# A two-layer encoder on one core: bank numbering in the down-projection, row norms in two steps, and transfers on another queue

## The chip, the cores and the metric

The kernel runs on one core of a Trainium2 chip as one program. The metric is the device time of one execution in microseconds; before the change the median of three runs is 3454.63 us (3453.96 to 3462.44).

## The reference

1024 tokens of width 1024 in float32, two layers. Each layer has four kinds of attention side by side (A dilated windows, B latent, C differential, D two-dimensional neighbourhoods), an output projection, a gated MLP of width 2816 with a convolution over three tokens, and a gated embedding. In short:

```python
for i in range(DEPTH):                                   # 2 layers
    hn = rms_norm(h, attn_norm[i])
    cols = hn @ w_in[i]                                  # 1024 -> A | B | C | D columns
    a_cols, b_cols, c_cols, d_cols = jnp.split(cols, split_at, axis=-1)
    o_a = dilated_mixture(rope(qa, pos), rope(ka, pos), va)
    o_b = mla_mixer(b_cols, mla_q_norm[i], w_uq[i], mla_kv_norm[i], w_ukv[i], pos)
    o_c = diff_mixer(c_cols, ..., diff_subln[i], lam_init, pos)   # (softmax1 - lam*softmax2) @ v, then rms_norm
    o_d = neighbourhood_attn(qd, kd, vd, na_rpb[i])      # windows of a 16 x 64 grid, with a bias table
    mix = jnp.concatenate([merge_heads(o) for o in (o_a, o_b, o_c, o_d)], axis=-1)
    h = h + mix @ w_o[i]
    hn = rms_norm(h, ffn_norm[i])
    u = dwconv_centred(hn @ w_up[i], conv_w[i], conv_b[i])        # 1024 -> 2 x 2816
    gate, val = jnp.split(u, 2, axis=-1)
    h = h + (jax.nn.gelu(gate) * val) @ w_down[i]        # 2816 -> 1024
    e = p[i] @ w_ple_proj[i]
    g = jax.nn.sigmoid(rms_norm(h, ple_norm[i]) @ w_ple_gate[i])
    h = h + g * e
return rms_norm(h, final_norm)
```

`rms_norm` divides a row by the root of its mean square and multiplies it by a gain.

## The kernel before

Tokens lie in NT = 8 tiles of 128 rows. A float32 product is made of three matmuls of rounded operands: each operand is split into a part `hi` and a remainder `lo` (`whi`, `wlo` of a weight by GpSimd, lines 111 and 112; `ah`, `al` of an activation by ScalarE and VectorE, lines 1242 and 1243; `xh`, `xl` of a transposed row, lines 162 and 163), and line 181 multiplies hi by hi, lo by hi and hi by lo. TensorE's results go to three kinds of banks, `psM`, `psT` (128 x 512, two of each) and `psS` (128 x 1024, two).

The MLP's down-projection takes the 2816 hidden columns as 11 chunks of two blocks of 128. For each chunk `down_tile` (line 1293) goes over the eight token tiles: twelve matmuls of 128 x 512 fill both halves of a bank, and VectorE adds them to `h` (line 1299). While one chunk is computed, `act_load` and `down_w` fetch and split the activations and weights of later ones. The last chunk (`down_last`) is joined with what follows: after its tile `t`, the row's norm is computed, its transpose follows, and then a quarter of the embedding's gate (`gate`, line 1321). At the end of a layer the last quarter of the gate is followed by the next layer's first norm, transpose and input projection, or, in the last layer, by the final norm and the store to `out`.

`norm_rows` (line 147) is a chain over three engines: ScalarE squares the row and sums it (line 149), GpSimd makes the reciprocal root (lines 137 and 139), VectorE scales the row (line 151); then TensorE transposes it (line 161). `norm_a` calls it, and `pipeline(n, *stages)` (line 999) writes out a list of functions as a software pipeline: in step `s`, stage `k` handles tile `s - k`.

The attention streams run beside the input projections. Differential attention (C) handles heads in two pairs; after the second head of a pair, GpSimd makes the pair's normalised output `c_ob` (line 450) and SP issues eight stores of it to the rows of `mix` in memory (line 453). Then the neighbourhood stream (D) loads two masks (lines 812 and 814), four bias tables `d_T` (line 825), to which VectorE adds a mask (line 826), and the tiles `d_x` (line 831), which TensorE transposes (line 835). GpSimd's queue already issues one kind of store, `mix<-b_ob` (line 569).

Pools, engines and dependencies are written by hand, but a framework schedules: it may place an instruction of an engine before others that were written earlier.

Of the kernel before, what the change touches and what calls it, by code (L numbers as in the profile page):

```python
# [19 lines left out]
P = 128  # L20
# [25 lines left out]
def kernel(ctx: ExitStack, tc: tile.TileContext, a, out, dbg=None):  # L46
# [19 lines left out]
    def small(n, name):  # L66
        return sm.tile([P, n], F32, name=name, tag=f"{name}_{n}")
# [77 lines left out]
        return g  # L145

    def norm_rows(ht, gB, hn):
        ss = small(1, "ss")
        se.activation(hn, ht, AF.Square, scale=1.0 / 32.0, accum_out=ss)  # L149
        r = rstd(ss, EPS, 1)  # L150
        ve.scalar_tensor_tensor(hn, ht, r[:, 0:1], gB, op0=ALU.mult, op1=ALU.mult)  # L151

    def transpose_split(src, hi, lo, nk, bank):

# [195 lines left out]
    def attn_C(c, L, cd, mix):  # L350
# [77 lines left out]
        def finish(h, g, st, turn):  # L428

            pair, hh = h // 2, h % 2  # L430
            if g == 0:
                st["ob"] = osp.tile([P, NT, 64], F32, name="oh", tag="oh")
            oh = st["ob"]
            turn(oh[:, 2 * g:2 * g + 2])
            if g < 3:
                return
            if hh == 0:
                obs[pair] = osp.tile([P, NT, 2, 64], F32, name="c_ob", tag="c_ob")
            ob = obs[pair]
            r1 = small(8, "r1")  # L440
            ve.reciprocal(r1, st["ss"])
            ge.tensor_tensor(oh, oh, r1.unsqueeze(2).to_broadcast([P, NT, 64]), op=ALU.mult)
            sq = ob[:, :, hh]
            ge.tensor_tensor(sq, oh, oh, op=ALU.mult)
            ss = small(8, "css")
            ve.tensor_reduce(ss, sq, op=ALU.add, axis=AX.X)
            ge.tensor_scalar(ss, ss, 1.0 / 64.0, None, op0=ALU.mult)
            r2 = rstd(ss, DIFF_EPS, NT)
            ge.tensor_tensor(oh, oh, r2.unsqueeze(2).to_broadcast([P, NT, 64]), op=ALU.mult)
            ge.tensor_tensor(ob[:, :, hh], oh, gsub.unsqueeze(1).to_broadcast([P, NT, 64]), op=ALU.mult)  # L450
            if hh == 1:
                for t in range(NT):
                    nc.sync.dma_start(mix[t][:, 512 + pair * P:512 + (pair + 1) * P],
                                      ob[:, t].rearrange("p h d -> p (h d)"))

        def V(h, kt):
            return pair_data[h // 2][2][:, kt, (h % 2) * 64:(h % 2 + 1) * 64]
# [347 lines left out]
    def attn_D(c, L, dd, mix):  # L805
# [3 lines left out]
        ptp = c.enter_context(tc.tile_pool(name="d_pt", bufs=3))  # L809
        op = c.enter_context(tc.tile_pool(name="d_o", bufs=2))  # L810
        cmask = tbp.tile([P, 64], F32, name="cmask")
        nc.sync.dma_start(cmask, a["cmask"])
        rmask = tbp.tile([P, 9], F32, name="rmask")
        nc.sync.dma_start(rmask, a["rmask"])
        T = tbp.tile([P, 4, 14, 64], F32, name="d_T")
        Ti = tbp.tile([P, 4, 9, 64], F32, name="d_Ti")
        qkh = tbp.tile([P, 4, S], F32R, name="d_qkh")
# [4 lines left out]
            return f"inB{L}" not in done or f"A{L}" in done  # L822

        def table(h):
            nc.sync.dma_start(T[:, h], skew[L][h])
            ve.tensor_tensor(T[:, h], T[:, h], cmask.unsqueeze(1).to_broadcast([P, 14, 64]), op=ALU.add)
            ve.tensor_tensor(Ti[:, h], T[:, h, 2:11], rmask.unsqueeze(2).to_broadcast([P, 9, 64]), op=ALU.add)

# [161 lines left out]

    def norm_a(pool, ht, gB):
        hn = pool.tile([P, D], F32, name="hn", tag="hn")
        norm_rows(ht, gB, hn)
        return hn

    def norm_b(hn, hi, lo, t):
        transpose_split(hn, hi, lo, KD, lambda: psS(t))
# [24 lines left out]
    with ExitStack() as c:  # L1022
        np_ = c.enter_context(tc.tile_pool(name="nrm", bufs=3))
        gp = c.enter_context(tc.tile_pool(name="gp", bufs=1))
        ring = WRing(c, "i0", 8, 2)
        stg = c.enter_context(tc.tile_pool(name="stg0", bufs=2))
        gB = gp.tile([P, D], F32, name="gB")

        ht = []
        for t in range(NT):  # L1030
            ht.append(np_.tile([P, D], F32, name="ht", tag="ht", bufs=NT))
            nc.sync.dma_start(ht[t], a["x"][t * P:(t + 1) * P])
            if t == 0:
                nc.sync.dma_start(gB, a["attn_norm"][0].partition_broadcast(P))
            if t == 1:
                Wi = {0: in_weights(0, 0, ring, False)}
            if t == 4:
                load_tables("cos32q", "sin32q")
        load_tables("cos32", "sin32", "cos64", "sin64")

        def first(t, _):
            if t == 4:
                Wi[1] = in_weights(0, 1, ring, False)
            return norm_a(np_, ht[t], gB)
        pipeline(NT, first, lambda t, hn: norm_b(hn, *xT[t], t),
                 lambda t, _: in_tile(0, 0, Wi[0], xT[t], t, stg, scr_d["C"]))
        for t in range(NT):
            in_tile(0, 1, Wi[1], xT[t], t, stg, scr_d["C"])
    src_h = [a["x"][t * P:(t + 1) * P] for t in range(NT)]
    for L in range(DEPTH):  # L1050
# [52 lines left out]
        with ExitStack() as c:  # L1103
# [23 lines left out]
            def proj(i, _):  # L1127
                t = tok(i)
                ht = ring.s.tile([P, 1024], F32, name="wst")
                nc.sync.dma_start(ht, hpart[t])  # L1130
                m = mp.tile([P, 256], F32, name="mixt", tag="mixt")
                nc.sync.dma_start(m, mix[t][:, 256:512])
                mh = mp.tile([P, 2, P], F32R, name="mh", tag="mh")
                ml = mp.tile([P, 2, P], F32R, name="ml", tag="ml")
                transpose_split(m, mh, ml, 2, lambda: psT(0))
                for n in range(2):
                    o = psM(n)
                    cs = slice(n * 512, (n + 1) * 512)
                    mm3(o, [((mh[:, k], ml[:, k]), (W[k][0][:, cs], W[k][1][:, cs])) for k in range(2)])
                    ve.tensor_tensor(ht[:, cs], o, ht[:, cs], op=ALU.add)  # L1140
                nc.sync.dma_start(hd1[t], ht)
                hn = row_tile("hn")
                norm_rows(ht, gB, hn)
                if i == NT - 1:
                    raw_load(0)
                return hn

            half = {}

            def turn(i, hn):  # L1150
# [33 lines left out]
                if i == NT - 2:  # L1184
                    prep(0, 0)
                    prep(0, 2)
            pipeline(NT, proj, None, turn)

        ap_ = c0.enter_context(tc.tile_pool(name="act", bufs=7))
        cu = ExitStack()  # L1190
# [96 lines left out]
        for t in range(NT):  # L1287
            nc.sync.dma_start(h[t], hd1[t])
        cf = ExitStack()
        np_ = cf.enter_context(tc.tile_pool(name="nrm", bufs=2))  # L1290

        def down_tile(t, ch):
            bank = (psM, psT, lambda n: psS(n)[:, :512])[t % 3 if ch < NC_ - 1 else 0]
            halves = [(bank(n), slice(n * 512, (n + 1) * 512)) for n in range(2)]
            outs = [(o, [(acts[f](t), (Ws[f][0][:, cs], Ws[f][1][:, cs])) for f in (2 * ch, 2 * ch + 1)])
                    for o, cs in halves]
            mm_side(outs)
            for o, cs in halves:
                ve.tensor_tensor(h[t][:, cs], o, h[t][:, cs], op=ALU.add)  # L1299
# [36 lines left out]
        with ExitStack() as c:  # L1336
            ep = c.enter_context(tc.tile_pool(name="plq", bufs=2))
            Wg = gate_weights(0)

            Wgs = {}  # L1340

            def down_last(t, _):
                down_tile(t, NC_ - 1)
                if t == NT - 1:
                    Wgs[1] = gate_weights(1)
                return norm_a(np_, h[t], gB)
            pipeline(NT, down_last, lambda t, hn: norm_b(hn, *x3[t], t), lambda t, _: gate(t, 0, Wg, ep))
        cf.close()
        with ExitStack() as c:
            np_ = c.enter_context(tc.tile_pool(name="nrm", bufs=2))  # L1350
            ep = c.enter_context(tc.tile_pool(name="plq", bufs=2))
            gN = load_gB(gp, a["final_norm"] if last else a["attn_norm"][L + 1])
            Wi = {}
            for q in (1, 2):
                for t in range(NT):
                    gate(t, q, Wgs[q], ep)
                    if t == 0:
                        Wgs[q + 1] = gate_weights(q + 1)
            xT = []
            if not last:  # L1360
                scr_d = scratch(L + 1)
                Wi[0] = in_weights(L + 1, 0, ring, True)

            def after(t, _):
                hn = norm_a(np_, h[t], gN)
                if last:
                    nc.sync.dma_start(out[t * P:(t + 1) * P], hn)
                else:
                    nc.sync.dma_start(hd2[t], h[t])
                return hn  # L1370

            def turn(t, hn):
                xT.append(new_xt(xtp))
                norm_b(hn, *xT[t], t)

            def nxt_in(t, _):
                in_tile(L + 1, 0, Wi[0], xT[t], t, stg, scr_d["C"])
                if t == NT - 2:
                    Wi[1] = in_weights(L + 1, 1, ring, True)
            pipeline(NT, lambda t, _: gate(t, 3, Wgs[3], ep), after, *(() if last else (turn, nxt_in)))  # L1380
            if not last:
                for t in range(NT):
                    in_tile(L + 1, 1, Wi[1], xT[t], t, stg, scr_d["C"])
# [68 lines left out]
```

## Time and profile before

| | |
|---|---|
| median of 3 runs | 3454.63 us |
| profiled execution | 3454.64 us, span of the instructions 3452.9 us |
| TensorE (PE) busy | 3221.7 us, 93% |
| weight loads (PEld) busy | 2681.2 us, 78% |
| VectorE (DVE) | 2079.8 us, 60% |
| ScalarE (ACT) | 1350.0 us, 39% |
| GpSimd (POOL) | 1390.0 us, 40% |
| mean traffic | 95 GB/s |

A row of the profile names an engine, a line of the kernel, an operation and its operands as out<-in. In a timeline, `[1.69 <-DVE h L1299]` behind a row says that the engine stood idle for 1.69 us and that the last thing that it waited for was VectorE's instruction of line 1299 on `h`. `x8` counts equal instructions in a row. The weight loads go beside the matmuls and are no work of their own on the path.

### The profile page before, as it was taken

How to read it: one execution, taken by the hardware profiler on the slowest of the kernel's cores; microseconds unless marked ns; L12 is line 12 of the kernel's file. 1: busy time of each engine (PE TensorE's matmuls, PEld its weight loads, DVE VectorE, ACT ScalarE, POOL GpSimd, SP SyncE). 2: the span in 40 equal slices, each digit the busy share in tenths (PEclk: the TensorE clock that was granted, in tenths of full speed). 3: DMA queues.
4: the chain of work that ended last, by engine and by line, in shares of the span. 5: the costliest groups of instructions: out<-in, count | busy, mean ns of one | idle time of the engine just before them, and what ended most of it. 6: DMA issues, size and time to landing. Idle time of an engine off the chain costs nothing. (4 is left out here: it accounts for less than half of the span.)

```text
span 3452.9 us, 50023 instructions
## 1 busy us (share of the span) xinstructions
PE 3221.7 (93%) x19088; PEld 2681.2 (78%) x19088; DVE 2079.8 (60%) x2898; ACT 1350.0 (39%) x2630; POOL 1390.0 (40%) x1318
## 2 busy tenths in 40 slices
PE   8999889998899999999999998899978999999988
PEld 8888778776677777777998888777756777777778
DVE  5677346645566667566547763465455666666664
ACT  3554247624444443002225543565344444420022
POOL 1532213202677775232325231132026777753232
PEclk9999999999899999999999999899998999999999
DMA  6211322324322224221341113223243222242222
GB/s 202 80 54 53 103 77 80 110 88 153 121 86 74 80 86 164 84 92 55 106 131 49 54 57 102 83 77 121 74 173 107 80 86 74 80 168 90 81 71 86
DMA packets 184544, 327.09 MB, mean 95 GB/s; under 512 B 34928, under 2 KB 119792, under 8 KB 184304
## 3 DMA queue, kind: packets, MB, share of 16 engines
q1 hardware_dynamic: 183280, 321.79, 28.8%
q8 instruction: 151, 2.47, 0.3%
q0 software_dynamic: 1024, 2.10, 0.2%
q14 instruction: 89, 0.73, 0.1%
HBM read 232.25 MB, written 95.22 MB: 95 GB/s over the span
## 5 line engine op out<-in xcount | busy, mean ns | idle before, releaser
L181 PE MATMUL psM<-whi,xh 128*128 128x256 f32 (+1 forms) x1408 | 369.6, 300 | 0.2 <-ACT pr_raw L232 0.2
L181 PE MATMUL psM<-whi,xl 128*128 128x256 f32 (+1 forms) x1408 | 360.2, 295 | 2.7 <-DVE xl L163 2.7
L181 PE MATMUL psM<-wlo,xh 128*128 128x256 f32 (+1 forms) x1408 | 357.6, 293 | 3.9 <-POOL wlo L112 3.9
L111 POOL TENSOR_SCALAR whi<-wst 128x1024 fp32r<-128x1024 f32 (+2 forms) x102 | 117.8, 1155 | 602.8 <-PE psT L181 350.0
L281 ACT ACTIVATE Prow<-psS,nm 128x1024 f32<-128x1024 f32 x192 | 214.3, 1117 | 196.1 <-DVE nm L279 194.6
L112 POOL TENSOR_TENSOR wlo<-wst,whi 128x1024 fp32r<-128x1024 f32 (+2 forms) x102 | 263.9, 2588 | 13.4 <-PE psT L1207 5.7
L279 DVE TENSOR_REDUCE nm<-psS 128x1 f32<-128x1024 f32 x192 | 230.5, 1217 | 48.0 <-PE psS L417 28.5
L181 PEld LDWEIGHTS psM<-whi,xh 128*128 128x128 f32 x1408 | 248.3, 193 | 8.1 <-ACT pr_raw L232 4.6
L181 PEld LDWEIGHTS psM<-wlo,xh 128*128 128x128 f32 x1408 | 248.6, 194 | 5.5 <-POOL wlo L112 5.4
L181 PEld LDWEIGHTS psM<-whi,xl 128*128 128x128 f32 x1408 | 249.0, 194 | 3.8 <-DVE xl L163 3.6
L1242 ACT CAST ah<-wst 128x1024 fp32r<-128x1024 f32 x44 | 46.4, 1055 | 388.6 <-PE psT L181 364.4
L1076 POOL TENSOR_TENSOR wsum<-wst 128x512 f32<-128x512 f32 x88 | 150.9, 1714 | 69.5 <-issue 69.0
L256 PE MATMUL psT<-identr,Prow 128*128 128x128 f32 x1024 | 150.2, 278 | 16.8 <-DVE Prow L423 11.2
L256 PEld LDWEIGHTS psT<-identr,Prow 128*128 128x128 f32 x1024 | 115.6, 141 | 62.4 <-issue 28.3
L1099 ACT CAST whl<-wsum 128x512 fp32r<-128x512 f32 x176 | 108.3, 618 | 139.0 <-PE psS L1207 124.4
L1099 ACT CAST whl<-wst 128x512 fp32r<-128x512 f32 x132 | 81.8, 621 | 195.2 <-PE psM L1207 169.2
L1212 DVE SCALAR_TENSOR_TENSOR ug<-G,cw,ug 128x1023 f32<-128x1023 f32 x44 | 59.6, 1354 | 163.1 <-ACT ug L1211 163.1
L1100 POOL TENSOR_TENSOR whl<-wst,whl 128x512 fp32r<-128x512 f32 x88 | 115.0, 1308 | 98.0 <-ACT whl L1099 98.0
L1226 POOL TENSOR_TENSOR uv<-ug,uv 128x1024 f32<-128x1024 f32 x44 | 117.7, 2676 | 76.4 <-DVE uv L1214 68.5
L566 POOL TENSOR_TENSOR b_ob<-oh,r 128x128 f32<-128x128 f32 x32 | 14.7, 458 | 310.4 <-DVE oh L274 309.5
L1100 POOL TENSOR_TENSOR whl<-wsum,whl 128x512 fp32r<-128x512 f32 x88 | 133.8, 1520 | 1.9 <-ACT whl L1099 1.9
L1299 DVE TENSOR_TENSOR h<-psM,h 128x512 f32<-128x512 f32 x152 | 97.7, 682 | 56.2 <-PE psM L181 55.8
(336 smaller groups left out, 9204.8 us busy)
## 6 DMA issues: line engine op xcount, KB each, us to landing
wst<-w_up SPq DMA_DIRECT2D x88, 512.0 KB, 3.8
v<-uv SPq DMA_DIRECT2D x44, 512.0 KB, 2.9
wst<-w_down SPq DMA_DIRECT2D x44, 512.0 KB, 3.4
wst<-v SPq DMA_DIRECT2D x44, 512.0 KB, 3.6
wst<-w_in SPq DMA_DIRECT2D x36, 512.0 KB, 3.6
wst<-w_o SPq DMA_DIRECT2D x16, 512.0 KB, 4.4
hp<-o_hx SPq DMA_DIRECT2D x16, 512.0 KB, 2.6
wst<-hp SPq DMA_DIRECT2D x16, 512.0 KB, 4.2
```

The source lines that it names most:

```text
L111: ge.tensor_scalar(hi, src, 1.0, 0.0, op0=ALU.mult, op1=ALU.add)
L112: ge.tensor_tensor(lo, src, hi.bitcast(F32), op=ALU.subtract)
L181: te.matmul(o, *ms[i], start=i == 0, stop=i == n - 1)
L256: te.transpose(t[:, i], src[:, (4 * c + i) * P:(4 * c + i + 1) * P], ident)
L279: ve.tensor_reduce(nm, s, op=ALU.max, axis=AX.X, negate=True)
L281: se.activation(p_, s, AF.Exp, bias=nm[:, 0:1], scale=1.0, accum_out=ssum)
L1076: ge.tensor_tensor(r, x, y, op=op)
L1099: se.copy(hi, src)
L1100: (ve if p % 2 else ge).tensor_tensor(lo, src, hi.bitcast(F32), op=ALU.subtract)
L1212: ve.scalar_tensor_tensor(u[:, 1:], x[:, :S - 1], cw[:, f, 0:1], u[:, 1:], op0=ALU.mult, op1=ALU.add)
L1226: ge.tensor_tensor(v, g, v, op=ALU.mult)
L1299: ve.tensor_tensor(h[t][:, cs], o, h[t][:, cs], op=ALU.add)
```

## The change

Three edits. (1) `down_tile` counts tiles over all chunks when it chooses the bank, where it counted within a chunk. (2) `norm_rows` returns a function that does the scaling; a new stage `scaled` (or `store` at the kernel's end) of the pipelines calls it, so that the scale of tile `t` is written out a step after its square, and the pool for the rows has three buffers instead of two at two places. (3) The stores of `c_ob`, the two masks and the four tables are issued by GpSimd (`ge`) instead of SP.

```diff
@@ -145,10 +145,15 @@
         return g
 
     def norm_rows(ht, gB, hn):
+
         ss = small(1, "ss")
         se.activation(hn, ht, AF.Square, scale=1.0 / 32.0, accum_out=ss)
         r = rstd(ss, EPS, 1)
-        ve.scalar_tensor_tensor(hn, ht, r[:, 0:1], gB, op0=ALU.mult, op1=ALU.mult)
+
+        def scale():
+            ve.scalar_tensor_tensor(hn, ht, r[:, 0:1], gB, op0=ALU.mult, op1=ALU.mult)
+            return hn
+        return scale
 
     def transpose_split(src, hi, lo, nk, bank):
 
@@ -450,8 +455,8 @@
             ge.tensor_tensor(ob[:, :, hh], oh, gsub.unsqueeze(1).to_broadcast([P, NT, 64]), op=ALU.mult)
             if hh == 1:
                 for t in range(NT):
-                    nc.sync.dma_start(mix[t][:, 512 + pair * P:512 + (pair + 1) * P],
-                                      ob[:, t].rearrange("p h d -> p (h d)"))
+                    ge.dma_start(mix[t][:, 512 + pair * P:512 + (pair + 1) * P],
+                                 ob[:, t].rearrange("p h d -> p (h d)"))
 
         def V(h, kt):
             return pair_data[h // 2][2][:, kt, (h % 2) * 64:(h % 2 + 1) * 64]
@@ -809,9 +814,9 @@
         ptp = c.enter_context(tc.tile_pool(name="d_pt", bufs=3))
         op = c.enter_context(tc.tile_pool(name="d_o", bufs=2))
         cmask = tbp.tile([P, 64], F32, name="cmask")
-        nc.sync.dma_start(cmask, a["cmask"])
+        ge.dma_start(cmask, a["cmask"])
         rmask = tbp.tile([P, 9], F32, name="rmask")
-        nc.sync.dma_start(rmask, a["rmask"])
+        ge.dma_start(rmask, a["rmask"])
         T = tbp.tile([P, 4, 14, 64], F32, name="d_T")
         Ti = tbp.tile([P, 4, 9, 64], F32, name="d_Ti")
         qkh = tbp.tile([P, 4, S], F32R, name="d_qkh")
@@ -822,7 +827,7 @@
             return f"inB{L}" not in done or f"A{L}" in done
 
         def table(h):
-            nc.sync.dma_start(T[:, h], skew[L][h])
+            ge.dma_start(T[:, h], skew[L][h])
             ve.tensor_tensor(T[:, h], T[:, h], cmask.unsqueeze(1).to_broadcast([P, 14, 64]), op=ALU.add)
             ve.tensor_tensor(Ti[:, h], T[:, h, 2:11], rmask.unsqueeze(2).to_broadcast([P, 9, 64]), op=ALU.add)
 
@@ -990,8 +995,10 @@
 
     def norm_a(pool, ht, gB):
         hn = pool.tile([P, D], F32, name="hn", tag="hn")
-        norm_rows(ht, gB, hn)
-        return hn
+        return norm_rows(ht, gB, hn)
+
+    def scaled(_, scale):
+        return scale()
 
     def norm_b(hn, hi, lo, t):
         transpose_split(hn, hi, lo, KD, lambda: psS(t))
@@ -1042,7 +1049,7 @@
             if t == 4:
                 Wi[1] = in_weights(0, 1, ring, False)
             return norm_a(np_, ht[t], gB)
-        pipeline(NT, first, lambda t, hn: norm_b(hn, *xT[t], t),
+        pipeline(NT, first, scaled, lambda t, hn: norm_b(hn, *xT[t], t),
                  lambda t, _: in_tile(0, 0, Wi[0], xT[t], t, stg, scr_d["C"]))
         for t in range(NT):
             in_tile(0, 1, Wi[1], xT[t], t, stg, scr_d["C"])
@@ -1140,10 +1147,10 @@
                     ve.tensor_tensor(ht[:, cs], o, ht[:, cs], op=ALU.add)
                 nc.sync.dma_start(hd1[t], ht)
                 hn = row_tile("hn")
-                norm_rows(ht, gB, hn)
+                scale = norm_rows(ht, gB, hn)
                 if i == NT - 1:
                     raw_load(0)
-                return hn
+                return scale
 
             half = {}
 
@@ -1184,7 +1191,7 @@
                 if i == NT - 2:
                     prep(0, 0)
                     prep(0, 2)
-            pipeline(NT, proj, None, turn)
+            pipeline(NT, proj, scaled, turn)
 
         ap_ = c0.enter_context(tc.tile_pool(name="act", bufs=7))
         cu = ExitStack()
@@ -1287,10 +1294,10 @@
         for t in range(NT):
             nc.sync.dma_start(h[t], hd1[t])
         cf = ExitStack()
-        np_ = cf.enter_context(tc.tile_pool(name="nrm", bufs=2))
+        np_ = cf.enter_context(tc.tile_pool(name="nrm", bufs=3))
 
         def down_tile(t, ch):
-            bank = (psM, psT, lambda n: psS(n)[:, :512])[t % 3 if ch < NC_ - 1 else 0]
+            bank = (psM, psT, lambda n: psS(n)[:, :512])[(NT * ch + t) % 3 if ch < NC_ - 1 else 0]
             halves = [(bank(n), slice(n * 512, (n + 1) * 512)) for n in range(2)]
             outs = [(o, [(acts[f](t), (Ws[f][0][:, cs], Ws[f][1][:, cs])) for f in (2 * ch, 2 * ch + 1)])
                     for o, cs in halves]
@@ -1344,10 +1351,10 @@
                 if t == NT - 1:
                     Wgs[1] = gate_weights(1)
                 return norm_a(np_, h[t], gB)
-            pipeline(NT, down_last, lambda t, hn: norm_b(hn, *x3[t], t), lambda t, _: gate(t, 0, Wg, ep))
+            pipeline(NT, down_last, scaled, lambda t, hn: norm_b(hn, *x3[t], t), lambda t, _: gate(t, 0, Wg, ep))
         cf.close()
         with ExitStack() as c:
-            np_ = c.enter_context(tc.tile_pool(name="nrm", bufs=2))
+            np_ = c.enter_context(tc.tile_pool(name="nrm", bufs=3))
             ep = c.enter_context(tc.tile_pool(name="plq", bufs=2))
             gN = load_gB(gp, a["final_norm"] if last else a["attn_norm"][L + 1])
             Wi = {}
@@ -1362,12 +1369,13 @@
                 Wi[0] = in_weights(L + 1, 0, ring, True)
 
             def after(t, _):
-                hn = norm_a(np_, h[t], gN)
-                if last:
-                    nc.sync.dma_start(out[t * P:(t + 1) * P], hn)
-                else:
+                scale = norm_a(np_, h[t], gN)
+                if not last:
                     nc.sync.dma_start(hd2[t], h[t])
-                return hn
+                return scale
+
+            def store(t, scale):
+                nc.sync.dma_start(out[t * P:(t + 1) * P], scale())
 
             def turn(t, hn):
                 xT.append(new_xt(xtp))
@@ -1377,7 +1385,7 @@
                 in_tile(L + 1, 0, Wi[0], xT[t], t, stg, scr_d["C"])
                 if t == NT - 2:
                     Wi[1] = in_weights(L + 1, 1, ring, True)
-            pipeline(NT, lambda t, _: gate(t, 3, Wgs[3], ep), after, *(() if last else (turn, nxt_in)))
+            pipeline(NT, lambda t, _: gate(t, 3, Wgs[3], ep), after, *((store,) if last else (scaled, turn, nxt_in)))
             if not last:
                 for t in range(NT):
                     in_tile(L + 1, 1, Wi[1], xT[t], t, stg, scr_d["C"])
```

What moves on the engines is seen at three places. VectorE at a boundary of two chunks of the down-projection, layer 1 (`h_29133` is token tile 0, `h_29140` tile 7), before:

```order
L1299 TENSOR_TENSOR h_29138<-psS,h_29138 128x512 x2
L1299 TENSOR_TENSOR h_29139<-psM,h_29139 128x512 x2
L1243 TENSOR_TENSOR al<-wst,ah 128x1024 x2
L1299 TENSOR_TENSOR h_29140<-psT,h_29140 128x512 x2
L1299 TENSOR_TENSOR h_29133<-psM,h_29133 128x512 x2
L1299 TENSOR_TENSOR h_29134<-psT,h_29134 128x512 x2
```

and after the change:

```order
L1306 TENSOR_TENSOR h_29138<-psM,h_29138 128x512 x2
L1306 TENSOR_TENSOR h_29139<-psT,h_29139 128x512 x2
L1250 TENSOR_TENSOR al<-wst,ah 128x1024 x2
L1306 TENSOR_TENSOR h_29140<-psS,h_29140 128x512 x2
L1306 TENSOR_TENSOR h_29133<-psM,h_29133 128x512 x2
L1306 TENSOR_TENSOR h_29134<-psT,h_29134 128x512 x2
```

The order is the same, with the two remainders ahead of tile 7's adds; tile 7 leaves bank T for bank S, which tile 2 of the next chunk takes, and tile 1 takes T from tile 6.

GpSimd after the second pair of differential heads in layer 1, before (`whi` and `wlo` are splits of the input projection's weights):

```order
L450 TENSOR_TENSOR c_ob<-oh,gsub 128x8x64
L111 TENSOR_SCALAR whi<-wst 128x1008
L112 TENSOR_TENSOR wlo<-wst,whi 128x1008
L111 TENSOR_SCALAR whi<-wst 128x672
L112 TENSOR_TENSOR wlo<-wst,whi 128x672
```

and after; between `c_ob` and the first row shown stand the stores of the first six tiles of `mix`:

```order
L458 DMA mix_6_15857<-c_ob 128x128
L458 DMA mix_7_15858<-c_ob 128x128
L817 DMA cmask<-cmask 128x64
L819 DMA rmask<-rmask 128x9
L830 DMA d_T<-skew_0_17174 128x896
L111 TENSOR_SCALAR whi<-wst 128x1008
L830 DMA d_T<-skew_1_17175 128x896
L112 TENSOR_TENSOR wlo<-wst,whi 128x1008
L111 TENSOR_SCALAR whi<-wst 128x672
L830 DMA d_T<-skew_2_17176 128x896
L112 TENSOR_TENSOR wlo<-wst,whi 128x672
L830 DMA d_T<-skew_3_17177 128x896
```

Eight stores, two masks and the first table stand ahead of the first split, and the other tables between the splits and behind them.

TensorE at the end of the last chunk in layer 1, before, from the last matmuls of the last token tile (`psM<-whi,al`) on; `psS<-identr,hn` are the transposes of a row, and `psT<-whi,xh` and the like are gate tiles:

```order
L181 MATMUL psM<-whi,al 128x512 x2
L161 MATMUL psS<-identr,hn 128x128 x8
L181 MATMUL psT<-whi,xh 128x256 x8
L181 MATMUL psT<-wlo,xh 128x256 x8
L181 MATMUL psT<-whi,xl 128x256 x8
L181 MATMUL psT<-whi,xh 128x256 x7
L161 MATMUL psS<-identr,hn 128x128 x8
L181 MATMUL psT<-whi,xh 128x256
```

and after:

```order
L186 MATMUL psM<-whi,al 128x512 x2
L166 MATMUL psS<-identr,hn 128x128 x8
L186 MATMUL psT<-whi,xh 128x256 x8
L186 MATMUL psT<-wlo,xh 128x256 x8
L186 MATMUL psT<-whi,xl 128x256 x8
L166 MATMUL psS<-identr,hn 128x128 x8
L186 MATMUL psT<-whi,xh 128x256 x8
L186 MATMUL psT<-wlo,xh 128x256 x8
L186 MATMUL psT<-whi,xl 128x256 x8
L166 MATMUL psS<-identr,hn 128x128 x8
```

Between the last matmuls on `al` and the last transposes of a row stood one transpose and a gate tile with seven further matmuls; now there are two transposes and two gate tiles.

## Rows read from the trace of the kernel before

**Rows 1.** The page: busy time, share and instructions by engine; granted clock in 40 slices.

```profile
PE 3221.7 (93%) x19088; PEld 2681.2 (78%) x19088; DVE 2079.8 (60%) x2898; ACT 1350.0 (39%) x2630; POOL 1390.0 (40%) x1318
...
PEclk9999999999899999999999999899998999999999
```

**Rows 2.** The list of waits: engine, tile and line, releaser; us in total, times, longest.

```profile
DVE d_T L826 <- DMA D<-pr_raw: 31.8, 2, 16.8
...
PE psT L181 <- DVE h L1299: 30.4, 18, 1.7
```

**Rows 3.** The chain of waits, down-projection, layer 1: start, us, what.

```profile
3143.69 2.81 PE psT L181 x11
...
3146.50 2.72 PE psS L181 x12
...
3167.83 2.35 PE psT L181 x9
```

**Rows 4.** Timeline of VectorE at a chunk boundary: start, us, work [idle before <-releaser].

```profile
3136.99 5.46 DVE L1243 TENSOR_TENSOR al<-wst,ah 128x1024 fp32r<-128x1024 f32 x2
3142.36 1.27 DVE L1299 TENSOR_TENSOR h<-psT,h 128x512 f32<-128x512 f32 x2
```

**Rows 5.** Timeline of TensorE at the same boundary.

```profile
3143.10 1.09 PE L181 MATMUL psT<-whi,ah 128*128 128x512 f32 x2 [1.69 <-DVE h L1299]
```

**Rows 6.** The tile `al`: least, median and longest ns of one, first and last start.

```profile
L1243 DVE TENSOR_TENSOR al<-wst,ah x44: 1225/2111/3427, 1340.3 to 3307.5; 128x1024 fp32r<-128x1024 f32 x44
```

**Rows 7.** Timeline of TensorE in the last chunk, layer 1.

```profile
3317.77 1.06 PE L161 MATMUL psS<-identr,hn 128*128 128x128 f32 x8 [2.30 <-DVE hn L151]
...
3357.21 1.11 PE L181 MATMUL psT<-whi,xl 128*128 128x256 f32 x8
...
3358.15 0.99 PE L181 MATMUL psT<-whi,xh 128*128 128x256 f32 x7
...
3363.01 1.06 PE L161 MATMUL psS<-identr,hn 128*128 128x128 f32 x8 [3.87 <-DVE hn L151]
```

**Rows 8.** Timeline of TensorE in layer 0: last chunk, end of the layer.

```profile
1649.21 1.94 PE L161 MATMUL psS<-identr,hn 128*128 128x128 f32 x8 [2.55 <-DVE hn L151]
...
1711.05 1.07 PE L161 MATMUL psS<-identr,hn 128*128 128x128 f32 x8 [2.13 <-DVE hn L151]
```

**Rows 9.** A stretch of it: length, busy PE, PEld, DVE, ACT, POOL; granted clock; DMA; GB/s.

```profile
1711.00:1718.00 7.00, 6.95 (x47) 6.98 (x48) 3.85 (x6) 4.22 (x8) 1.36 (x4) 0.76 0.45 171
```

**Rows 10.** Timeline of all engines at the end of the kernel.

```profile
3439.27 1.28 DVE L151 SCALAR_TENSOR_TENSOR hn<-h,rs_r,gB 128x1024 f32<-128x1024 f32 x1 [1.43 <-POOL rs_r L139]
...
3443.34 1.06 ACT L149 ACTIVATE hn<-h 128x1024 f32<-128x1024 f32 x1 [2.62 <-DMA out<-hn]
...
3445.48 1.28 DVE L151 SCALAR_TENSOR_TENSOR hn<-h,rs_r,gB 128x1024 f32<-128x1024 f32 x1 [1.60 <-POOL rs_r L139]
...
3447.97 1.28 DVE L151 SCALAR_TENSOR_TENSOR hn<-h,rs_r,gB 128x1024 f32<-128x1024 f32 x1 [1.21 <-POOL rs_r L139]
```

**Rows 11.** The store `mix<-b_ob` of line 569, already issued by GpSimd: ns of one; landing.

```profile
L569 POOL DMA_DIRECT2D mix<-b_ob x32: 543/563/793, 673.0 to 2536.7; - x32
...
DMA to landing us min/median/max: 1.9/2.6/4.6
```

**Rows 12.** Timeline of SP after the second pair, layer 0.

```profile
354.03 3.64 SPq L453 DMA_DIRECT2D mix<-c_ob  x8
```

**Rows 13.** Timeline of GpSimd after the first pair, layer 0.

```profile
273.41 1.05 POOL L111 TENSOR_SCALAR whi<-wst 128x1024 fp32r<-128x1024 f32 x1 [28.00 <-PE psM L181]
```

**Rows 14.** Timeline of GpSimd at the end of the second pair, layer 0.

```profile
352.71 1.28 POOL L450 TENSOR_TENSOR c_ob<-oh,gsub 128x512 f32<-128x512 f32 x1
```

**Rows 15.** Timeline of TensorE after the second pair, layers 0 and 1.

```profile
358.57 0.42 PE L181 MATMUL psM<-wlo,xh 128*128 128x336 f32 x1 [0.63 <-POOL wlo L112]
...
371.24 1.08 PE L835 MATMUL psT<-identr,d_x 128*128 128x128 f32 x4 [4.61 <-DMA d_x<-D]
...
2083.31 0.63 PE L835 MATMUL psT<-identr,d_x 128*128 128x128 f32 x4 [2.58 <-DMA d_x<-D]
```

## Prediction

> **What bounds the kernel now.** I read the shares by engine first [rows 1]. TensorE is busy 3221.7 of the 3452.9 us span and its clock is granted in full nearly everywhere, so a change that removes no matmul can win only from the other 231 us, in which TensorE stands. The list of waits comes next [rows 2]: matmuls into bank T wait 30.4 us for the down-projection's adds, 18 times, at most 1.7. Then come the chain of waits around two of the 18 [rows 3] and the timelines of VectorE and TensorE at one [rows 4, 5]: the reader is to see a period of 24.1 us for eight tiles that need 8 x 2.72 = 21.76. For the norms I read what TensorE waits for a normalised row [rows 7 to 9] and the kernel's end [rows 10]; for the moved transfers, what stands on the queues of GpSimd and SP and who waits for it [rows 11 to 15].
>
> **Banks.** A chunk has eight tiles. Numbered anew in each chunk, they go M,T,S,M,T,S,M,T and then M,T again, so tile 1 of a chunk takes the bank of tile 7 of the chunk before, two tiles later instead of three. Just there VectorE makes two activation remainders (`al`, 5.46 us for both) ahead of tile 7's adds. These start at 3142.36, and TensorE's first matmul into T, at 3143.10, has waited 1.69 us [rows 4, 5]. The loss is larger than the wait, since the first pair afterwards takes 1.09 us: the chain starts that tile at 3143.69 and the next of its kind at 3167.83 [rows 3], 24.14 us apart and 2.38 more than eight tiles take. With nine such boundaries in each of two layers, the 18 of [rows 2], that is 18 x 2.38 = 42.8 us.
>
> Counted over all chunks, a bank comes back after three tiles at a boundary too. VectorE's order keeps the two remainders ahead of tile 7's adds; only the banks' names change. Tile 7's bank is then wanted by tile 2 of the next chunk, which begins at 3146.50 in [rows 3] and would at about 3144.1 without the lost 2.38. The adds are done at 3142.36 + 1.27 = 3143.6, half a microsecond earlier. Bounds: a remainder takes at most 3.43 us in the trace [rows 6], and two of these would put the adds 1.4 us later and leave a wait of 0.9 at each boundary, so the gain is at least 18 x (2.38 - 0.9) = 27; nothing lost at all, 43. Since 5.46 is already the sum of a median (2.11) and a longest one, I take 42.8. The last chunk uses bank M alone before and after, and 80 tiles leave the same last banks ahead of it: 0.
>
> **Norm scale in a step of its own.** The framework reorders what is emitted, so the order on the engines counts. In the output projection the three engines keep their order, and at the kernel's start one scale changes places with a neighbour on VectorE, for which TensorE's order does not change: 0 for both. Four places are left.
>
> - Last chunk, layer 1. The first transpose waits 2.30 us [rows 7]; it stays so, as the first scale still stands ahead of the next adds. The following one may wait 0.4 longer. Row 7's transpose waits 3.87. Between the last projection tile and it stood one transpose, a gate tile and seven matmuls; now two transposes and two gate tiles do. Groups of eight gate matmuls start 0.94 apart [rows 7], so a gate tile is 2.83 and the cover grows by 0.8 + 2.83 - 0.83 = 2.8. A wait of about 1.1 is left, for the same scale. A wait of that size also costs clock: in layer 0, after one of 2.13 us, the granted clock is 0.76 over the next 7 us [rows 8, 9], which loses 1.7. So -2.8 - 1.7 + 0.4 = -4.
> - Last chunk, layer 0: the same with a wait of 2.55 [rows 8], of which some 1.1 stays: -1.5 - 1.7 + 0.4 = -3.
> - End of layer 0. Row 0's transpose, with its 2.13 us and its lost clock, comes one gate tile (2.83) later, which covers it: -2.1 - 1.7 = -3.8.
> - End of kernel. Row 6's square waits 2.62 us for a store to free its buffer [rows 10]; a third buffer takes that away. But two scales now follow each other ahead of gate tile 6's adds. Row 4's scale stays at 3439.27; then come, with the rows' durations, scale 1.2, scale 1.2, two adds 0.9, square to scale 2.3, scale 1.2, adds 0.9, square to scale 2.3: row 7's scale at 3449.3 instead of 3447.97, +1.3.
>
> Together -9.5. Bounds: -15 if none of these waits is left, +3 if they only move and the end costs two scales more.
>
> **Transfers on GpSimd's queue.** In each layer sixteen stores of differential rows, two masks and four tables go from SP to GpSimd. A store of the same size takes GpSimd 543 to 793 ns, 563 at the median, and lands in 2.6 us [rows 11]; SP issues eight in 3.64 us [rows 12]. The first pair's eight fall into 28 us in which GpSimd waits for TensorE [rows 13]: 0. The second pair's product ends at 352.71 + 1.28 = 353.99 [rows 14], and 8 + 2 + 1 issues of 0.563, 6.2 us, now stand ahead of the next weights' split, two more tables between the splits. TensorE waits for these splits already, 0.63 us at 358.57 and again for the next [rows 15], so only what TensorE's new order puts there, matmuls of the next tile and transposes, hides the delay. I take 7 us of waiting per layer and 1.7 for the clock. What SP no longer issues it gives back: its `d_x` transfers go out some 4 us earlier, and the waits for them, 4.61 us in layer 0 and 2.58 in layer 1 [rows 15], end, with their 1.7 of clock. So layer 0: 8.7 - 0.6 - 4.6 - 1.7 = +1.8, layer 1: 8.7 - 0.6 - 2.6 - 1.7 = +3.8, less about 1.8 in each for smaller waits of these two kinds: +2 in all. The tables are issued at about the old time, and VectorE stands 16.8 us ahead of the first [rows 2]: 0. Bounds: -6 if the interleaved matmuls cover most of the splits' delay, +14 if the `d_x` waits stay too.
>
> In the trace GpSimd's stores stay under 0.8 us [rows 11]. The Trainium skill ("SBUF — State Buffer", section "SBUF: two separate sides") says that a transfer issued from GpSimd is starved while VectorE copies within SBUF in its two-port mode, and gives about 3.1 us instead of 0.62. By that, an estimate, the 24 transfers of the second pairs would cost 60 us more, and the change would lose. Against it here: VectorE stands idle for 16.8 us at the second pair [rows 2].
>
> **Sum.** The profiled execution took 3454.6 us (span 3452.9 and 1.7 around it), like the median of the runs, 3454.63, so nothing is scaled: 3454.6 - 42.8 - 9.5 + 2 = 3404 us.
>
> **Rivals.**
> 1. The stall moves instead of going: tile 2 waits 0.9 us in place of tile 1, 3454.6 - 27 - 9.5 + 2 = 3420. For it: the margin is half a microsecond; against it: the row holds a remainder of the longest kind already.
> 2. The second pairs' issues cost the upper bound and the norm step gives nothing: 3454.6 - 42.8 + 14 = 3426. For it: the splits are waited for now.
> 3. Everything is covered: 3454.6 - 43 - 15 - 6 = 3391. For it: TensorE's order has changed at each of these waits.
> 4. Slower: GpSimd is held until a transfer lands. Twelve transfers in each layer stand ahead of weights for which TensorE waits; at c us each instead of 0.56 TensorE loses 24 x (c - 0.56) more. With 50 us won elsewhere this decides from c = 2.65, close to the median landing; at the longest landing, 4.6 [rows 11], the time is 3404 + 24 x 4.04 = 3501. Against it: 32 such issues never took over 0.8. The page of the Trainium skill named above points this way.
> 5. The bank is not what limits: some other part of the boundary keeps its 24.1 us, 3454.6 - 9.5 + 2 = 3447. Against it: the wait names the adds, and only bank T has it 18 times.
>
> **Numbers.** A measurement of this kernel can tell about 0.3%, 10 us, from no change. Forecast 0.68, rival 1 0.12, rival 2 0.08, rival 3 0.07, rival 4 0.02, rival 5 0.03. The forecast and rivals 1 to 3 are faster by over 10 us, 0.95; rival 5 is within, 0.03; rival 4 is slower, 0.02. The forecast's own bounds, some 10 us either way from the norms and the queue, hold most of this; the range takes in rival 1 and half of 2 and 3, and leaves out 4 and 5: 3393 to 3422.
>
> **What would show it.** Right: a chain in the down-projection with 21.8 us for eight tiles, no adds among TensorE's waits but in the last chunk, row 7's transpose waiting about 1 us there, 44 more issues of 0.55 us on GpSimd, the second pairs' weight splits 6 us later, and TensorE waiting for these instead of for `d_x`. Wrong: 18 waits for adds that now name another bank; issues of over 1 us on GpSimd; VectorE standing ahead of a table while TensorE waits for VectorE; a last scale that is later against the last gate tile by much more than 1.3 us.

## The result and the profile after

The changed kernel takes 3409.06 us at the median (3406.30 to 3414.97, five runs) against 3454.63 before; the ratio is 0.9865, with a 95% interval of 0.985 to 0.9881, some 46 us less. 3404 us were forecast. The page's engine line and granted clock:

```profile
PE 3205.9 (94%) x19088; PEld 2678.6 (79%) x19088; DVE 2077.6 (61%) x2898; ACT 1349.7 (40%) x2630; POOL 1415.2 (42%) x1362
...
PEclk9999999999799999999999998999998999999999
```

TensorE executes the same 19088 matmuls [rows 1]; the span is shorter by 45.6 us, of which its busy time gives 15.8 and its idle time the rest. GpSimd has 44 instructions more.

The chain of waits in the down-projection of layer 1 (start, us, what) answers to [rows 3]:

```profile
3105.49 2.72 PE psM L186 x12
3108.20 2.72 PE psT L186 x12
3110.93 2.72 PE psS L186 x12
3113.64 2.72 PE psM L186 x12
3116.36 2.72 PE psT L186 x12
3119.09 2.72 PE psS L186 x12
```

It holds nothing but TensorE. A chunk begins at 3113.48 in TensorE's timeline; around it stand, on VectorE [rows 4] and then on TensorE [rows 5]:

```profile
3111.94 5.45 DVE L1250 TENSOR_TENSOR al<-wst,ah 128x1024 fp32r<-128x1024 f32 x2
3117.32 1.27 DVE L1306 TENSOR_TENSOR h<-psS,h 128x512 f32<-128x512 f32 x2
```

```profile
3118.92 0.62 PE L186 MATMUL psS<-whi,ah 128*128 128x512 f32 x2
```

VectorE is as late as before. But tile 7's adds end at 3117.32 + 1.27 = 3118.59, and tile 2 takes that bank at 3118.92, without idle time and without a slow first pair.

With the first matmuls of chunks, streams and stages as marks on TensorE's timeline (the C stream is the differential attention, the A stream the dilated one), the 45.6 us of the span are made up so:

| stretch | layer 0 | layer 1 |
|---|---|---|
| start, to the C stream | -0.6 | |
| attention, projections, up-projection | +2.8 | +4.7 |
| ten chunks of the down-projection | -24.5 | -24.5 |
| last chunk and end of the layer | -1.1 | -2.4 |

At the second pair of differential heads, GpSimd's timeline in layer 0 [rows 14] reads:

```profile
352.99 4.33 POOL L458 DMA_DIRECT2D mix<-c_ob  x8 [0.29 <-POOL c_ob L455]
357.32 0.55 POOL L817 DMA_DIRECT2D cmask<-cmask  x1
357.86 0.55 POOL L819 DMA_DIRECT2D rmask<-rmask  x1
358.40 0.55 POOL L830 DMA_DIRECT2D d_T<-skew  x1
359.02 1.03 POOL L111 TENSOR_SCALAR whi<-wst 128x1008 fp32r<-128x1008 f32 x1
```

and TensorE's there, and in layer 1 [rows 15]:

```profile
360.10 0.65 PE L186 MATMUL psM<-whi,xh 128*128 128x336 f32 x1 [3.64 <-POOL whi L111]
...
376.58 1.09 PE L840 MATMUL psT<-identr,d_x 128*128 128x128 f32 x4 [3.07 <-DMA d_x<-D]
```

```profile
2070.41 0.87 PE L840 MATMUL psT<-identr,d_x 128*128 128x128 f32 x3 [3.65 <-DMA d_x<-D]
```

The issues cost 0.54 us each. The weight split is late, as it was forecast to be, but TensorE still waits for a `d_x`.

In the last chunk of layer 1 [rows 7] row 7's transpose waits 1.00 us instead of 3.87:

```profile
3316.06 1.06 PE L166 MATMUL psS<-identr,hn 128*128 128x128 f32 x8 [1.00 <-DVE hn L154]
```

At the end of layer 0 the transpose of row 0 waits no more [rows 8], and the first projection tile waits in its place:

```profile
1691.98 0.36 PE L186 MATMUL psM<-whi,xh 128*128 128x256 f32 x1 [1.33 <-ACT xh L167]
...
1694.45 0.58 PE L186 MATMUL psM<-whi,xl 128*128 128x256 f32 x1 [2.00 <-DVE xl L168]
```

The windows behind it [rows 9] (us, busy of PE, PEld, DVE, ACT and POOL, granted clock, DMA share, GB/s) show the clock at its lower level for six microseconds:

```profile
1694.00:1700.00 6.00, 5.55 (x26) 5.56 (x27) 4.36 (x8) 3.10 (x5) 1.65 (x4) 0.50 0.62 221
```

And at the kernel's end [rows 10] VectorE's last scales:

```profile
3389.61 1.28 DVE L154 SCALAR_TENSOR_TENSOR hn<-h,rs_r,gB 128x1024 f32<-128x1024 f32 x1 [1.43 <-POOL rs_r L139]
3391.64 1.28 DVE L154 SCALAR_TENSOR_TENSOR hn<-h,rs_r,gB 128x1024 f32<-128x1024 f32 x1 [0.75 <-POOL rs_r L139]
...
3400.24 1.28 DVE L154 SCALAR_TENSOR_TENSOR hn<-h,rs_r,gB 128x1024 f32<-128x1024 f32 x1 [2.21 <-POOL rs_r L139]
```

From row 4's scale to row 7's it is 10.6 us where it was 8.7.

### The profile page after: what moved, and what is told of

Read it like the earlier page. It is cut to its first block, busy times and chain, and to the rows that moved or that the text cites. A ratio compares the mean times of both kernels' runs of the same rounds, so it can differ in the third digit from the quotient of the medians.

```text
span 3407.3 us, 50062 instructions
## 1 busy us (share of the span) xinstructions
PE 3205.9 (94%) x19088; PEld 2678.6 (79%) x19088; DVE 2077.6 (61%) x2898; ACT 1349.7 (40%) x2630; POOL 1415.2 (42%) x1362
## 5 line engine op out<-in xcount | busy, mean ns | idle before, releaser
L1106 ACT CAST whl<-wsum 128x512 fp32r<-128x512 f32 x176 | 108.4, 618 | 138.9 <-PE psS L1214 122.1
L1214 PE MATMUL psS<-t4h,whl 128*128 128x512 f32 x352 | 120.7, 404 | 8.6 <-DVE V L1269 8.6
```

The source lines that it names most:

```text
L1106: se.copy(hi, src)
L1214: te.matmul(banks[z], *m, start=first and i == 0, stop=i == len(ms) - 1, skip_group_check=True)
```

## The experiments

**One edit at a time.** The kernel before with one edit each, and the changed kernel without the queue edit.

```diff
 # e1: banks alone            (also in the changed kernel)
-[t % 3 if ch < NC_ - 1 else 0]
+[(NT * ch + t) % 3 if ch < NC_ - 1 else 0]
 # e2: queue alone            (e4: the changed kernel with sync back)
-nc.sync.dma_start(...)   # mix<-c_ob, cmask, rmask, d_T<-skew
+ge.dma_start(...)
 # e3: norm alone             (the hunks on norm_rows, scaled, store and the pools)
```

> The kernel before with the bank count alone. By the traces the ten chunks ahead of the last take 242.3 us before and 217.8 after in each layer, so the theory (the bank's distance is the whole cost of the boundary) expects 49 us less, about 3405.6, and in the trace a chunk period of 21.76 us at every boundary. By the prediction's own sum it would be 42.8 less, 3411.8. The rival (part of the gain at the boundaries is made by the other two edits) expects a gain well under 42, 3415 or more.

> The kernel before with the stores, masks and tables issued by GpSimd alone. From the traces (PE at the first projection tile of group B to the start of the A group, layer 0 and 1) the theory expects it slower by 5 to 8 us, 3460 to 3462; the prediction's sum says 2 us slower, 3456.6. The rival (the relieved SP queue pays for it elsewhere) expects the same or faster, 3452 or less.

> The kernel before with the norm split and the third row buffers alone. The traces (last chunk to the end of each layer: 211.8 to 210.6 us in layer 0, 143.9 to 141.5 in layer 1, start 0.6) make the theory expect about 4 us less, 3450.5. The prediction's sum says 9.5 less, 3445. The rival (the split only moves waits) expects no change, 3454 or more.

> The changed kernel with the stores, masks and tables back on SP: banks and norm split together. The theory expects the changed kernel less the queue's loss of 5 to 8 us: 3401 to 3404. The prediction's sum says 2 us less than the changed kernel, 3407. The rival (the queue edit helps) expects more than the changed kernel's 3409.

| run | ratio to before | interval | us |
|---|---|---|---|
| banks alone | 0.9867 | 0.9851 to 0.9883 | -46 |
| queue alone | 1.0023 | 1.0013 to 1.0033 | +8 |
| norm alone | 1.0005 | 0.9994 to 1.0016 | +2, -2 to +6 |
| banks and norm | 0.9859 | 0.9844 to 0.9874 | -49 |

The banks make the gain by themselves. Ten chunks take 217.8 us in each layer of that run, with eight tiles every 21.76 us, as in the changed kernel. The queue edit alone is a loss, clear of zero. The norm edit can't be told from nothing, where 9.5 us were forecast.

The three single edits add up to -36 us, and the changed kernel has -46. By time the queue's 8 us don't show beside the banks: the ratio is 0.9865 with that edit and 0.9859 without, and the intervals overlap. The traces show it all the same: from the C stream's first matmul to the A stream's, both layers together, it takes 782 to 784 us in the four profiles with the whole queue edit and two buffers for `d_x` (the changed kernel, e2, e5, e6) and 772 to 776 in the six without (before, e1, e3, e4, e9, e10).

**What about the bank decides.** The changed kernel with two banks in turn, so that every bank comes back after two tiles; and with the remainder written twice, which was meant to double VectorE's work at the boundary.

```diff
 # e5
-bank = (psM, psT, lambda n: psS(n)[:, :512])[(NT * ch + t) % 3 if ch < NC_ - 1 else 0]
+bank = (psM, psT)[t % 2 if ch < NC_ - 1 else 0]
 # e6, in act_load
 ve.tensor_tensor(lo, v, hi.bitcast(F32), op=ALU.subtract)
+ve.tensor_tensor(lo, v, hi.bitcast(F32), op=ALU.subtract)
```

> The changed kernel, but with the tiles of the first ten chunks on two banks in turn (M,T,M,T,...), so that every bank comes back after two tiles, at the boundaries too. The theory (two tiles are too few there, three enough) expects the whole loss of the kernel before to come back, 18 stalls of 2.4 us or more, 43 to 52 us over the changed kernel: 3452 to 3461, with 1.7 us waits for the adds at every boundary. The rival (it was the irregular change of banks at a boundary, or bank T being written by two neighbours) expects no stall with a regular turn, 3409.

> The changed kernel with the activation remainder in the down-projection written twice by VectorE (the second writes the same values), so that VectorE has twice the 5.5 us at a boundary. The theory (VectorE's lateness eats the 0.5 us of margin) expects waits of about 1 us for the adds at most boundaries, 15 to 30 us over the changed kernel: 3424 to 3439. The rival (with three tiles between, what VectorE does at a boundary has no price) expects 3409, no adds in the list of waits.

With two banks the median is 3464.08 us (ratio 1.0022, 1.0012 to 1.0032): the whole loss is back, and what is over the time before is about what the queue edit costs alone. Ten chunks take 242.8 and 242.6 us, where they took 242.2 and 242.3 before. Its list of waits has the row of [rows 2] again, and in the second to the tenth chunk no tile waits but tile 1, which follows the remainders:

```profile
PE psT L186 <- DVE h L1306: 31.5, 20, 1.7
```

So it is the distance of two tiles where VectorE is late, and not the irregular turn. With the remainder written twice the kernel takes 3452.26 us (0.9988, 0.9979 to 0.9998), 43 more than the changed one, above the 15 to 30 expected, and not for the expected reason. The chain of waits:

```profile
3164.33 2.05 DVE al L1250
3166.37 0.02 issue
3166.40 3.31 DVE al L1251
3169.71 0.04 issue
3169.75 0.73 PE psS L186 x2
```

TensorE waits 1.5 us for the remainder itself, which the next chunk's second block reads, and in the second to the tenth chunk never for a bank. A chunk takes 23.6 us, which makes 35 of the 43. But the edit did not double what stands ahead of tile 7's adds: the framework put one block's remainder and its repeat there (2.12 and 3.30 us, in sum 5.4 as without the edit) and the other block's two behind those adds. So this run shows that the operand is the next limit behind the bank, where the theory had put the bank; what a later VectorE would do to the third bank is not shown.

**Stores or tables.** The changed kernel with one half of the queue edit taken back.

```diff
 # e7: stores on GpSimd, masks and tables on SP
-ge.dma_start(cmask, ...); ge.dma_start(rmask, ...); ge.dma_start(T[:, h], skew[L][h])
+nc.sync.dma_start(...)
 # e8: masks and tables on GpSimd, stores on SP
-ge.dma_start(mix[t][...], ...)
+nc.sync.dma_start(mix[t][...], ...)
```

> The changed kernel with the masks and tables back on SP; only the stores of differential rows go out from GpSimd. The theory (each issue on GpSimd ahead of the weight splits delays TensorE by its 0.55 us, eight of the twelve are stores) expects most of the queue's 8 us to stay, some 5 us over banks and norm split together, 3407 to 3410 here. The rival (the tables are what costs, since they stand between the splits and come late for VectorE) expects about 3404 to 3405.

> The changed kernel with the stores back on SP; only the masks and tables go out from GpSimd. The theory expects a small part of the queue's loss, some 2 to 3 us over banks and norm split together, 3404 to 3407. The rival (the tables are what costs) expects the changed kernel's 3409 to 3412.

The ratios are 0.9872 (0.9852 to 0.9892) and 0.9864 (0.9846 to 0.9882): by time the two can't be told apart, nor from the changed kernel, so how the loss is divided stays open. From the C stream to the A stream e7 takes 775.6 us, like the kernels without the edit, and e8 778.8, with one profile of each.

**The ends of the layers.** Banks and split with the transfers on SP, but the norm in one step after the last quarter of the gate; and the split there with an empty step before the projection.

```diff
 # e9 (with two row buffers there)
-scale = norm_a(np_, h[t], gN)
+hn = norm_a(np_, h[t], gN)()
-*((store,) if last else (scaled, turn, nxt_in))
+*(() if last else (turn, nxt_in))
 # e10
+*((store,) if last else (scaled, turn, None, nxt_in))
```

> Banks and the norm split, transfers on SP, but at the end of each layer (after the last quarter of the gate) the norm in one step with two buffers as before. The theory (there the split only turns the transpose's wait into waits for the split row, and the last scale comes later) expects the same time as banks and split together, within 3 us, with TensorE waiting some 2 us for the first row's transpose again and not for xh and xl of the first projection tile. The rival, the prediction's own term (3.8 us won at the end of layer 0, 1.3 lost at the kernel's end), expects 2.5 us more.

> Banks and the norm split, transfers on SP, with an empty pipeline step between the transpose and the first projection at the end of layer 0. The theory (the first projection tile waits 1.4 us for xh and 2.0 for xl of a row that was transposed just before it, because ScalarE and VectorE have the next rows' squares and scales ahead) expects these waits and the lost clock behind them to go, 3 to 5 us less than banks and split together, seen between the last chunk and the end of the layer's projection. The rival (the scheduler's order is set by the engines and not by the steps, or all of it is ScalarE's pace) expects no change.

One step at the ends gives 3400.81 us (0.984, 0.9826 to 0.9854), better than banks and full split (0.9859), with intervals that just overlap; the traces say that the split loses at the ends. From the last chunk to the next layer's C stream it takes 206.8 us, with the full split 211.8, before 211.8. The part of this behind the last chunk, from the gate's last quarter on, takes 105.8 to 107.0 us in the five profiles with one step there (before, e1, e2, e9, e12) and 108.4 to 111.3 in the eight with the split there (all others but e10). Row 0's transpose waits again:

```profile
1685.93 1.06 PE L166 MATMUL psS<-identr,hn 128*128 128x128 f32 x8 [2.14 <-DVE hn L154]
```

but the clock stays at 1.00 behind it. Of the five profiles with one step it falls there only in that of before, for 3.4 us; in the eight with the split it falls each time, for 3.4 or 6.8 us. So e9 wins more than the 3 us that were allowed for, and the rival, the prediction's own term, has the wrong sign. The empty step takes the two waits away and puts others in their place, 3.5 us for `xl` before a later transpose among them; the ratio is 0.986 (0.9845 to 0.9875), no change.

**The wait for d_x.** The changed kernel with a third buffer for `d_x`; then the parts that paid, together: e9 with that buffer.

```diff
 # e11: on the changed kernel; e12: on e9
-name="d_ld", bufs=2  ...  name="d_p", bufs=4
+name="d_ld", bufs=3  ...  name="d_p", bufs=3
```

> The changed kernel with three buffers instead of two for the tiles d_x, and three instead of four for the neighbourhood scores d_P to make room. The theory (a tile d_x is fetched only when TensorE has transposed the tile before the last, so moving other issues off SP can't end the wait for it) expects the waits for d_x (3.1 and 3.7 us) to fall below 1 and with the clock behind them 5 to 8 us less than the changed kernel, 3401 to 3404. The rival (SP's order, weights and rows of group B ahead of d_x, sets the wait) expects the waits to stay at 3 us and 3409.

> Banks, norm split without the layers' ends, transfers on SP, and three buffers for d_x (three for d_P): the parts that paid, together. If the gains are independent, the third buffer takes the waits for d_x (4.5 and 2.4 us) and their clock off the kernel with the norm in one step at the ends, 3401 less 5 to 9: 3392 to 3396. The rival (with the transfers on SP the d_x waits are set by SP's queue and not by the buffer) expects 3400.

The third buffer brings 3398.33 us (0.9843, 0.9822 to 0.9863, which overlaps the changed kernel's 0.985 to 0.9881); from the C stream to the A stream it takes 774.9 us instead of 783.4. The wait of 3.07 us in layer 0 becomes two:

```profile
374.47 0.63 PE L840 MATMUL psT<-identr,d_x 128*128 128x128 f32 x4 [0.46 <-issue]
...
377.65 0.63 PE L840 MATMUL psT<-identr,d_x 128*128 128x128 f32 x4 [1.78 <-DMA d_x<-D]
```

In sum that is 2.2 us and not below 1, and in layer 1 it is 3.3, so the theory of the buffer holds only in part: SP still issues the `d_x` that is waited for behind the rows of group B, as the rival has it. But behind these the clock stays at 1.00, where the changed kernel had 0.57 over the four us that hold its wait's end (first row; second row with the third buffer):

```profile
376.00:380.00 4.00, 3.42 (x16) 3.19 (x16) 0.96 (x3) 1.29 (x4) 0.00 (x0) 0.57 0.26 70
```

```profile
377.00:381.00 4.00, 3.35 (x23) 2.80 (x23) 1.51 (x4) 1.78 (x6) 0.00 (x0) 1.00 0.39 134
```

All together, e12 takes 3386.39 us (3385.70 to 3392.81; ratio 0.9811, 0.9798 to 0.9825), 68 us less than before and the fastest of all. It gains 14 us on e9 by the medians and 10 by the ratios, each to runs of the kernel before beside it, where 5 to 9 were expected. In its trace one `d_x` tile still waits 2.04 us for something that the trace does not name, and the next limit at the neighbourhood tiles is the bank that they are transposed into:

```profile
373.20 0.63 PE L840 MATMUL psT<-identr,d_x 128*128 128x128 f32 x4 [2.41 <-DVE d_qkl L846]
```

From the C stream's start to the A stream's, the two layers together take 5.6 us less than in e9; the other 8 or 9 us are spread over later stretches, and whether the buffers or the clock made them was not tried.

## Why the prediction was right, and which terms were not

The time lay in the range, and the mechanism that was to carry it did. Three terms were off and nearly cancelled, so that it is in part luck that the sum came within 5 us.

- **Banks, -42.8: mechanism right, size too small.** The traces give -49.0 (2 x 24.5); by time the banks alone have -46 (-40 to -51), which does not tell the two sizes apart. The prediction multiplied one boundary's 2.38 us by 18. In the trace of before 14 of the 18 cost that; four cost 4.0. There the clock fell after the stall, in the profile of before at the first boundary of layer 0 for instance (the columns are those of the windows above):

```profile
1379.00:1383.00 4.00, 3.36 (x9) 2.44 (x10) 2.28 (x4) 0.00 (x0) 3.43 (x2) 0.75 0.73 254
```

  14 x 2.38 + 4 x 4.0 = 49.3. The margin, 0.5 in the prediction, is 0.33. Rival 1 (the stall moves to tile 2) and rival 5 are refuted by the chain and by the run with banks alone. Half of rival 2 came true, since the norm step gave little and the queue lost 8 of its 14 us; the banks' larger gain hid it. Rival 3 did not happen: TensorE still waits for splits and for `d_x`.

- **Norm, -9.5: the step that failed is the end of layer 0.** The last chunk did as forecast: row 7's transpose waits 1.00 us (1.1 forecast) in layer 1 and 0.56 in layer 0, and the chunk with the gate's first quarter takes 4.3 and 4.6 us less in the profile after than in that of before (3 and 4 forecast). But "which covers it: -3.8" looked at the transpose alone. What is late next is the split of the transposed row: ScalarE and VectorE have the next rows' squares, scales and adds ahead of `xh` and `xl`. The 2.1 us came back as 1.33 + 2.00, and the clock was at its lower level for 6.8 us where it had been for 3.4; instead of 3.8 us won, the profiles above show some 3.5 us lost there. The kernel's end costs 1.9 where 1.3 were forecast; the nine profiles with the full split have the same 10.6 us from row 4's scale to row 7's, while e9, the queue alone and the banks alone have the old 8.7. By the traces the norm's sum is thus -4.3 - 4.6 + 3.5 + 1.9 = -3.5; by time it is +2 alone (-2 to +6) and -3 beside the banks, with intervals that overlap.

- **Queue, +2: the step that failed is "the waits for `d_x` end".** The split's delay was right in place and smaller than reckoned. The first split begins at 359.02, 4.0 us later than before:

```profile
355.05 1.03 POOL L111 TENSOR_SCALAR whi<-wst 128x1008 fp32r<-128x1008 f32 x1 [1.05 <-PE psM L181]
```

  TensorE waited 3.6 us for `whi` and 0.3 for `wlo`, not 7, since its new order had work for it. For the `d_x` that the prediction meant, the third tile, it was right too: it went out at 361.63 instead of 365.04, and TensorE no longer waits for it. But the wait went over to the fourth tile, 3.07 and 3.65 us. That one went out later, not 4 us earlier. SP's timeline in layer 0, before and then changed:

```profile
365.04 0.38 SPq L831 DMA_DIRECT2D d_x<-D  x1
...
368.11 4.56 SPq L831 DMA_DIRECT2D d_x<-D  x2
```

```profile
361.63 0.32 SPq L836 DMA_DIRECT2D d_x<-D  x1
...
366.65 0.90 SPq L125 DMA_DIRECT2D wst<-w_in  x2
368.54 2.18 SPq L238 DMA_DIRECT2D B<-pr_raw  x2
370.81 8.62 SPq L836 DMA_DIRECT2D d_x<-D  x4
```

  The fourth tile stands behind two weight loads and two stores of group B's rows, and its buffer comes free with TensorE's transposes of the second tile, which begin at 369.68 (at 366.03 before), so that the queue and the buffer released it within a few tenths of a microsecond. With a third buffer the tile that is waited for is the fifth; it too stands behind the B rows (372.57), but one tile more was there by then. With the tables back on SP (e7) the waits were 0.2 and 0.5. Both limits are real, and how much each weighs stays open. Measured alone, the edit costs 8 us (4 to 11).

- **Rival 4** (GpSimd held until a transfer lands) did not happen: the 32 stores took 0.54 to 0.78 us each and the eight tables 0.55 to 0.59. In layer 0 the first pair's stores were issued while VectorE was working, at 244 to 249 us, but on reductions and products and not on a copy. So no run here shows the price that the Trainium skill ("SBUF — State Buffer", section "SBUF: two separate sides") gives for a transfer issued from GpSimd beside a copy that VectorE makes within SBUF.

## What to carry to other kernels

When work rotates over a few banks, count the rotation over the whole loop and look at the place where the consumer is late: one tile more of distance was worth 46 of 3455 us here, while all else stayed as it was. When a step is moved out of a wait, follow the moved row two consumers further, on every engine, before the wait is booked as a gain. When issues leave a queue, read the new order of that queue and the buffers of what is left on it, before the remaining transfers are booked as earlier.

## What the runs showed of the hardware that was not expected

The same stall of 1.69 us was followed by a lower granted clock at some boundaries and not at others: in the three profiles with the old banks and nine stalls to a layer it was the first boundary of each layer and one later one, between the sixth and the eighth. A similar dip begins some 2.5 to 4 us behind the A stream's first matmul in both layers of all fourteen profiles; it lasts 3.4 us in some and 10.2 in most, and the longer one lengthens a stretch of 31 us there by some 3. So a wait's price in the trace of one execution is known to about 1.6 us, and TensorE's busy time fell by 15.8 us with the same matmuls.
